# Five instead of four pairs of contraction tiles by seven products, in ten weight pairs of a two-layer trunk

## The chip, the cores and the metric

The kernel runs on one core of a Trainium2 chip. The metric is the device time of one execution in microseconds (us). The kernel before takes 1144.99 us, the median of three runs (1144.73 to 1146.62).

## The reference

The program computes two layers on x of 256 positions by 2048 columns, all in float32. Layer 1 normalizes x, projects it to three blocks of 4096 columns (u, v and a gate), mixes v over positions and projects back; layer 2 does the same with q, k, v and a gate (2048 columns each) and a causal attention.

```python
def gmlp_branch(xn, w_in, v_g, w_s, b_s, w_out):
    proj = xn @ w_in                                  # 2048 x 12288
    uv = jax.nn.gelu(proj[..., :2 * GMLP_WIDTH])
    zg = proj[..., 2 * GMLP_WIDTH:]
    u, v = jnp.split(uv, 2, axis=-1)
    v = rms_norm(v, v_g)
    ws = w_s * causal[None]
    mixed = einsum('gts,bnsgc->bntgc', ws, vc) + bias
    y = u * mixed * jax.nn.silu(zg)
    return y @ w_out                                  # 4096 x 2048

def stick_breaking_branch(xn, w_in, w_out):
    proj = xn @ w_in                                  # 2048 x 8192
    q, k, v, zg = jnp.split(proj, 4, axis=-1)
    o = stick_breaking_attention(q, k, v)
    return (o * jax.nn.silu(zg)) @ w_out              # 2048 x 2048

def reference(x, ...):
    h = x
    for i in range(2):
        h = h + branch_i(rms_norm(h, norm_g[i]), ...)
    return rms_norm(h, final_g)
```

## The kernel before, in words

**Tiles and cuts.** A product of activations with weights contracts over tiles of 128 rows of the weight matrix (16 of them where 2048 rows are contracted, 32 where 4096 are); its output is 128 positions by 512 columns, one PSUM bank, and the 256 positions are two halves (t = 0 and 1). Float32 operands go through TensorE as two float32r parts. `cut` (L108) makes them for up to two contraction tiles of 512 columns: ScalarE casts the raw tile to the high half `hi` (L114), VectorE subtracts this from the raw tile and writes the low half `lo` (L115). Two tiles are 128 x 1024 elements in one instruction, a single one 128 x 512. The halves lie in a pool of five buffers each. `terms` (L118) then issues three matmuls of 128 x 512: left high by hi (L119), left high by lo (L120), left low by hi (L121). A contraction tile for one half of the positions is thus three matmuls.

**Pairs.** The weights are worked on in pairs of column blocks of 512 (class `Pair`, L233): two v blocks, or the u and gate blocks that belong together, or q and k. Of the contraction tiles, `HALVES` puts some in a first half (0, 1, 2, 3, 8) and as many in a second (4, 5, 6, 7, 9). With positions, contraction halves and column blocks that gives a 2 x 2 by 2 x 2 block product, done by the seven products of a Strassen-Winograd scheme instead of eight. A pair's number `ks` (4 or 5) says how many tiles of each half take part: with 4 the groups are two of two tiles, with 5 there is a third group of one tile, the fifth tile. The seven products are called p1 to p7 and are worked off in the order p1, p5, p6, p2, p7, p3, p4. Each needs a cut per group and then 3 x `ks` matmuls. They go into banks called a, e, b, a, c, b and d, in that order.

In the code `b11` and `b12` are the first half's tiles of the first and second column block, `b21` and `b22` those of the second half. In the names of the instruction rows below, tiles are numbered from zero and groups last: `gu2_b00_1` is B11 of the third u/gate pair, group 1; `b01` is B12, `b10` B21, `b11` B22; group `_2` is the fifth tile. `gu2_p12_lo` is the low half of product p1, group 2.

Between the products the sums of weight tiles are made: two subtractions per group on VectorE (L286: B12 - B11 after p1, and B21 less the running sum after p6), one addition of B22 (L314, for groups 0 and 1), and additions of weight tiles from DRAM by accumulating DMAs from GpSimd's queue (`plus`, L294): B22 onto B12, and with a fifth tile also B22's fifth tile onto the running sum that p6 reads. `others` (L264) later loads the fifth tiles of B21 and B22 into the pool of plain raw tiles. VectorE also adds e into b and c (L334, L342).

The contraction tiles outside the halves (`rest`, 8 of 16 for four tiles, 6 for five) are done plainly, first for column block 0 (`column(0)`, within the pair), then for column block 1 (`column(1)`): per two tiles one load into a pool of three raw buffers (`wraw`), one cut, and 12 matmuls for both halves of the positions. The names are `gu2_010_raw` for column block 0, tiles 10 and 11, and `gu2_110_raw` for column block 1. `run` (L373) spreads the column 1 of a pair over the products p1, p5 and on of the next pair, so that the plain cuts of the one stand between the product cuts of the other. After a column's last matmul `evac` reads out its two banks.

**Left sides.** p5, p6, p7 and p3 take sums of the activations in place of a block. `Left.sums` (L134) makes them for four tiles per half, `Left.fifth` (L158) for the fifth: four VectorE additions of 128 x 128 per half and position (L165), four subtractions (L167 to L170), a cast, and one low half 128 x 512 (L172). Its intermediate sums are in two scratch buffers, `sg0` (`_full`) and `sg1` (`_sm`). For x they are called s0e and xs0e, and they are queued at the middle of the last v pair (L539); for the second layer's input xs1e, queued when the first column block of the o2 pair is done (L777).

**Order of the stages.** First a plain double block of v (pair 0), then v pairs 1 to 3 (named v2, v4, v6), eight u/gate pairs (gu0 to gu7) with the mixing of v between (`mixing`, L592: 6 matmuls more per pair, and VectorE's vl, L611, and wl, L605), the output projection (op0, o0, op1, o2), then q/k and v pairs of layer 2 (qk0 to qk3, bv0, bv2), two gate pairs and the last projection f. Of these, gu3, gu5 and the pairs from o2 on have five tiles, but for qk0, which has four; v1 to v3 and the other u/gate pairs have four.

**The order on each engine.** The program text gives the data flow; a list scheduler with a timeline model (`schedule_with_timeline_sim`) decides each engine's order at build time. Nearly all weight loads go through SyncE's queue (SP, L223), in the order in which they were scheduled, and each waits there until its target buffer is free, so that one late buffer holds up all loads behind it. Fifth tiles that `load` takes with `behind` follow the load before them. Two steps of the text concern the change further: for u/gate pairs `fifth_first=True` (L648, L244) puts the fifth group first in p1 and p5 and in the sums between (in all others it comes last), and qk0's head runs beside o2's column 1, seven steps of which go ahead (L815).

## Time and profile before

| what | value |
|---|---|
| median of three runs | 1144.99 us |
| profiled execution, span | 1142.0 us |
| TensorE matmul (PE) busy | 1132.3 us, 99% of the span, 5168 matmuls |
| TensorE weight load (PEld) busy | 937.6 us, 82% |
| VectorE (DVE) busy | 1010.9 us, 89%, 1111 instructions |
| ScalarE (ACT) busy | 828.5 us, 73%, 1102 instructions |
| GpSimd (POOL) busy | 99.8 us, 9% |
| DRAM read | 259.55 MB, with writes 231 GB/s over the span |

The span is the profiled execution's own time from its first to its last instruction; the median of the runs lies 3.0 us above it. The granted TensorE clock shows 1.00 in the windows that are quoted. In the windows that follow, a number stands for the busy time of an engine in that stretch, with the number of instructions behind the x. A row of the groups view gives an engine, an operation and its tiles, the count, the busy time with the mean of one in ns, and the idle time of the engine ahead of these instructions with what ended it. A row of the waits view is a waiting instruction, an arrow, what it waited for, and three numbers: the total wait in us, the number of waits, and the longest.

The eight u/gate pairs begin p7 (the first product into bank c) at 185.1, 227.2, 269.4, 313.8, 353.0, 397.5, 436.7 and 478.8 us, the three v pairs at 62.5, 103.5 and 144.3 us, and qk0 at 699.9 us.

### The profile page before, as it was taken

What the parts mean: (1) busy time and instruction counts of PE and PEld (TensorE: products, weight loads), DVE (VectorE), ACT (ScalarE), POOL (GpSimd) and SP (SyncE); (2) the same over time, 40 slices, a digit from 0 to 9 for tenths busy, and PEclk for the clock granted to TensorE, in tenths of its full rate; (3) what the DMA queues carried; (4) which work ended last, traced back from release to release, by engine and by line L of the source; (5) the groups of instructions that cost most, each with busy time, mean ns of one, the idle gap of its engine ahead of it and who ended that gap; (6) DMA issues with size and microseconds to landing.
All of it is one profiled execution on the core that took longest, in us unless ns stands there. A gap on an engine that the chain in (4) does not pass through costs nothing.

```text
span 1142.0 us, 14838 instructions
## 1 busy us (share of the span) xinstructions
PE 1132.3 (99%) x5168; PEld 937.6 (82%) x5168; DVE 1010.9 (89%) x1111; ACT 828.5 (73%) x1102; POOL 99.8 (9%) x106
## 2 busy tenths in 40 slices
...
GB/s 335 317 290 270 214 252 270 194 266 241 173 274 249 191 261 240 177 296 142 267 259 166 276 203 282 153 280 211 181 283 200 211 230 174 272 88 241 325 225 92
DMA packets 135659, 264.72 MB, mean 232 GB/s; under 512 B 8992, under 2 KB 9504, under 8 KB 135456
## 3 DMA queue, kind: packets, MB, share of 16 engines
...
q8 instruction: 40, 0.66, 0.2%
...
HBM read 259.55 MB, written 4.19 MB: 231 GB/s over the span
## 4 chain that ended last, share of the span: by engine, by line
PE 93%; DMA 2%; DVE 2%; issue 1%; ACT 1%; SPq 0%; POOLq 0%; POOL 0%; ACTq 0%; DVEq 0%
PE gu_a L119 3%; PE gu_b L119 3%; PE gu_b L121 3%; PE gu_a L121 3%; PE gu_a L120 3%; PE gu_b L120 3%; PE op_acc L119 2%; PE op_acc L120 2%; PE op_acc L121 2%; PE gu_d L119 2%; PE gu_d L121 2%; PE gu_c L121 2%; PE gu_d L120 2%; PE gu_c L119 2%; PE gu_c L120 2%; PE qk_a L121 1%
## 5 line engine op out<-in xcount | busy, mean ns | idle before, releaser
L114 ACT CAST gu_p_hi<-gu_b 128x1024 fp32r<-128x1024 f32 (+1 forms) x126 | 122.9, 1004 | 38.4 <-DVE gu_b L314 16.1
L115 DVE TENSOR_TENSOR gu_p_lo<-gu_b,gu_p_hi 128x1024 fp32r<-128x1024 f32 (+1 forms) x126 | 142.8, 1165 | 1.9 <-ACT gu_p_hi L114 1.2
L115 DVE TENSOR_TENSOR qk_p_lo<-qk_b,qk_p_hi 128x1024 fp32r<-128x1024 f32 (+1 forms) x77 | 80.8, 1073 | 8.9 <-ACT qk_p_hi L114 8.4
L114 ACT CAST qk_p_hi<-qk_b 128x1024 fp32r<-128x1024 f32 (+1 forms) x77 | 70.5, 934 | 19.0 <-DMA qk_b<-in_b_w_in 4.0
L115 DVE TENSOR_TENSOR gu_lo<-gu_raw,gu_hi 128x1024 fp32r<-128x1024 f32 x60 | 72.1, 1218 | 12.5 <-ACT gu_hi L114 12.2
L114 ACT CAST gu_hi<-gu_raw 128x1024 fp32r<-128x1024 f32 x60 | 62.0, 1052 | 21.0 <-DMA gu_raw<-in_a_w_in 11.5
L115 DVE TENSOR_TENSOR v_lo<-v_raw,v_hi 128x1024 fp32r<-128x1024 f32 (+1 forms) x41 | 48.9, 1193 | 15.2 <-ACT v_hi L114 15.2
L114 ACT CAST v_hi<-v_raw 128x1024 fp32r<-128x1024 f32 (+1 forms) x41 | 41.7, 1028 | 27.9 <-DMA v_raw<-in_a_w_in 26.4
L115 DVE TENSOR_TENSOR v_p_lo<-v_b,v_p_hi 128x1024 fp32r<-128x1024 f32 x42 | 50.3, 1220 | 3.3 <-ACT v_p_hi L114 3.1
L114 ACT CAST v_p_hi<-v_b 128x1024 fp32r<-128x1024 f32 x42 | 43.0, 1049 | 9.8 <-PE v_c L121 4.9
L115 DVE TENSOR_TENSOR bg_p_lo<-bg_b,bg_p_hi 128x1024 fp32r<-128x1024 f32 (+1 forms) x42 | 42.5, 1041 | 4.8 <-ACT bg_p_hi L114 4.7
L114 ACT CAST o_p_hi<-o_b 128x1024 fp32r<-128x1024 f32 (+1 forms) x35 | 33.4, 965 | 18.1 <-PE op_acc L121 13.0
L115 DVE TENSOR_TENSOR bv_p_lo<-bv_b,bv_p_hi 128x1024 fp32r<-128x1024 f32 (+1 forms) x42 | 42.5, 1040 | 3.8 <-ACT bv_p_hi L114 3.6
L114 ACT CAST bv_p_hi<-bv_b 128x1024 fp32r<-128x1024 f32 (+1 forms) x42 | 37.4, 908 | 10.0 <-DMA bv_b<-in_b_w_in 3.0
L294 POOL DMA_DIRECT2D gu_b<-in_a_w_in x20 | 23.0, 1155 | 240.2 <-DVE gu_b L286 134.3
L114 ACT CAST bg_p_hi<-bg_b 128x1024 fp32r<-128x1024 f32 (+1 forms) x42 | 37.3, 907 | 8.0 <-PE bg_a L121 2.5
L115 DVE TENSOR_TENSOR o_p_lo<-o_b,o_p_hi 128x1024 fp32r<-128x1024 f32 (+1 forms) x35 | 38.3, 1113 | 5.4 <-ACT o_p_hi L114 5.4
L286 DVE TENSOR_TENSOR gu_b<-gu_b,gu_b 128x1024 f32<-128x1024 f32 (+1 forms) x36 | 41.4, 1169 | 0.1
L114 ACT CAST o_hi<-o_raw 128x1024 fp32r<-128x1024 f32 x22 | 23.0, 1052 | 24.9 <-DMA o_raw<-in_a_w_out 24.8
L115 DVE TENSOR_TENSOR o_lo<-o_raw,o_hi 128x1024 fp32r<-128x1024 f32 x22 | 26.7, 1221 | 15.2 <-ACT o_hi L114 15.0
L114 ACT CAST op_hi<-op_raw 128x1024 fp32r<-128x1024 f32 x24 | 25.1, 1053 | 19.3 <-PE op_acc L121 8.8
L120 PE MATMUL op_acc<-op_lo,yc 128*128 128x512 f32 x96 | 37.8, 393 | 0.0
...
## 6 DMA issues: line engine op xcount, KB each, us to landing
...
```

What stands on the lines that cost most here:

```text
L114: nc.scalar.copy(hi[:, sl], raw[:, sl])
L115: low[0] = nc.vector.tensor_sub(lo[:, sl], raw[:, sl], f(hi[:, sl]))
L119: nc.tensor.matmul(acc, lh, hi, start=first, stop=False, skip_group_check=True)
L120: nc.tensor.matmul(acc, lh, lo, start=False, stop=False, skip_group_check=True)
L121: nc.tensor.matmul(acc, ll, hi, start=False, stop=last, skip_group_check=True)
L286: nc.vector.tensor_sub(into[g], b0[g], b1[g])
L294: adds.append(nc.gpsimd.dma_start(into[g], self.src(HALVES[i][k], n, j), accum_op=ALU.add))
```

## The change

Ten pairs go from four to five tiles per half: the v pairs 1 to 3 (`KS_A`), six of the eight u/gate pairs (`KS_GU`), and qk0. The left sums that go with four tiles stay as they are; the fifth sums of x, xs0e, are no longer queued in the last v pair but made right after the first four, ahead of v pair 1. The small pool `exg`, in which a pair's fifth tiles of B11 and B12 land, is opened ahead of the v pairs and closed behind the u/gate pairs. qk0 takes for its fifth tiles the scratch buffers `sg0` and `sg1`, as the o pairs do, and five instead of seven steps of o2's column 1 go ahead of its head.

```diff
@@ -17,8 +17,8 @@
 NEVER = -1e30
 CB = 512
 WARM = 9
-KS_A = 4
-KS_GU = (4, 4, 4, 5, 4, 5, 4, 4)
+KS_A = 5
+KS_GU = (5, 5, 5, 5, 5, 5, 5, 5)
 KS_B = 5
 KS_O = 5
 KS_F = 5
@@ -535,8 +535,6 @@
     def mid_v(b, pair):
         for i in (b - 2, b - 1):
             gain(i, pair)
-        if b == NV - 2:
-            queue.append((1, x_fifth))
 
     def x_fifth():
         with tc.issue_after(ins_of(low[0])):
@@ -557,7 +555,10 @@
         if i < 3:
             square(2 + 2 * i)
             square(3 + 2 * i)
-    left.sums(KS_A, home("xs", [P, 2, 4, KS_A, P], F32R, "xs0"), "s0")
+    left.sums(4, home("xs", [P, 2, 4, 4, P], F32R, "xs0"), "s0")
+    x_fifth()
+    lx = ctx.enter_context(ExitStack())
+    ex = lx.enter_context(tc.tile_pool(name="exg", bufs=1))
     pending.append(p0.column(1))
     prior.append(KD // 4)
     for b in range(2, NV, 2):
@@ -585,7 +586,6 @@
         return py.tile([P, 2, 2, S], F32R, tag="yc3", bufs=2, name=f"yc3_{k2}")
 
     with ExitStack() as lg:
-        ex = lg.enter_context(tc.tile_pool(name="exg", bufs=1))
         pb = lg.enter_context(tc.tile_pool(name="pb", bufs=2))
         rv = None
 
@@ -649,6 +649,7 @@
         flush()
         drain()
         prior.clear()
+    lx.close()
     pv.close()
 
     hs = ctx.enter_context(tc.tile_pool(name="hs", bufs=1, space=bass.MemoryType.DRAM)).tile([P, NT, D], F32, name="hs")
@@ -810,9 +811,10 @@
     tail = p.column(1)
     while len(queue) > TPB // 2:
         queue.pop(0)[1]()
-    p = Pair(columns(b_w_in, 0, D), left1, KD, "qk0", 4, lambda j, t, bank: evac_qk(0, j, t, bank),
-             mid=lambda pair: drain())
-    for _ in range(7):
+    p = Pair(columns(b_w_in, 0, D), left1, KD, "qk0", KS_B, lambda j, t, bank: evac_qk(0, j, t, bank),
+             mid=lambda pair: drain(),
+             fifth=lambda j, name: jk.tile([P, 1, CB], F32, tag=f"sg{j}", bufs=1, name=name))
+    for _ in range(5):
         next(tail)
     drain()
     for _ in p.head():
```

Per converted pair, the seven products grow from 84 to 105 matmuls and from 14 cuts to 21 (14 of two tiles, 7 of one); the rest shrinks from 8 tiles to 6, 96 matmuls to 72 and 8 cuts to 6. Two subtractions of 128 x 512 come on VectorE (L286), two accumulating DMAs of 256 KB on GpSimd's queue (L294), and four loads of one tile (256 KB) in place of two loads of two (512 KB).

Three places show how the order moves. **The first** is SyncE's queue between two u/gate pairs. Before, between gu1 and gu2, both of four tiles:

```order
L223 DMA gu1_08_raw_2127<-in_a_w_in 128x2x512
L223 DMA gu1_010_raw_2145<-in_a_w_in 128x2x512
L223 DMA gu1_012_raw_2163<-in_a_w_in 128x2x512
L223 DMA gu2_b10_0_2340<-in_a_w_in 128x2x512
L223 DMA gu2_b10_1_2342<-in_a_w_in 128x2x512
L223 DMA gu2_b01_0_2209<-in_a_w_in 128x2x512
L223 DMA gu2_b01_1_2211<-in_a_w_in 128x2x512
L223 DMA gu2_b11_0_2270<-in_a_w_in 128x2x512
L223 DMA gu2_b11_1_2272<-in_a_w_in 128x2x512
L223 DMA gu2_b00_0_2205<-in_a_w_in 128x2x512
L223 DMA gu2_b00_1_2207<-in_a_w_in 128x2x512
L223 DMA gu1_014_raw_2181<-in_a_w_in 128x2x512
```

With the change, at the turn from gu2 to gu3, both of five tiles:

```order
L223 DMA gu3_b10_0_2842<-in_a_w_in 128x2x512
L223 DMA gu3_b10_1_2844<-in_a_w_in 128x2x512
L223 DMA gu2_012_raw_2686<-in_a_w_in 128x2x512
L223 DMA gu3_b01_0_2736<-in_a_w_in 128x2x512
L223 DMA gu3_b01_1_2738<-in_a_w_in 128x2x512
L223 DMA gu3_b11_0_2786<-in_a_w_in 128x2x512
L223 DMA gu3_b11_1_2788<-in_a_w_in 128x2x512
L223 DMA gu2_014_raw_2704<-in_a_w_in 128x2x512
L223 DMA gu3_b00_0_2730<-in_a_w_in 128x2x512
L223 DMA gu3_b00_1_2732<-in_a_w_in 128x2x512
L223 DMA gu3_b01_2_2734<-in_a_w_in 128x512
L223 DMA gu3_b00_2_2728<-in_a_w_in 128x512
```

The third plain load of column 0 (before `gu1_012_raw`, now `gu2_014_raw`) moved from ahead of the next pair's loads to behind its second tile of B22 (`gu3_b11_1`); the next pair's two fifth tiles stand at the end of its head's loads.

On VectorE at the same turn, before (gu1 to gu2):

```order
L605 TENSOR_TENSOR wl1_2107<-ws1_2104,wh1_2106 128x256
L115 TENSOR_TENSOR gu1_08_lo_2130<-gu1_08_raw_2127,gu1_08_hi_2129 128x1024
L115 TENSOR_TENSOR gu1_010_lo_2148<-gu1_010_raw_2145,gu1_010_hi_2147 128x1024
L115 TENSOR_TENSOR gu1_012_lo_2166<-gu1_012_raw_2163,gu1_012_hi_2165 128x1024
L611 SCALAR_TENSOR_TENSOR vl2_2467<-v0_113,nv_r_1739,vh2_2466 128x512 x2
L115 TENSOR_TENSOR gu1_014_lo_2184<-gu1_014_raw_2181,gu1_014_hi_2183 128x1024
L115 TENSOR_TENSOR gu2_p10_lo_2215<-gu2_b00_0_2205,gu2_p10_hi_2214 128x1024
L115 TENSOR_TENSOR gu1_18_lo_2227<-gu1_18_raw_2224,gu1_18_hi_2226 128x1024
L286 TENSOR_TENSOR gu2_b00_0_2205<-gu2_b01_0_2209,gu2_b00_0_2205 128x1024
```

and now (gu2 to gu3):

```order
L605 TENSOR_TENSOR wl2_2648<-ws2_2645,wh2_2647 128x256
L115 TENSOR_TENSOR gu2_p42_lo_2638<-gu2_b00_2_2348,gu2_p42_hi_2637 128x512
L115 TENSOR_TENSOR gu2_010_lo_2671<-gu2_010_raw_2668,gu2_010_hi_2670 128x1024
L115 TENSOR_TENSOR gu2_012_lo_2689<-gu2_012_raw_2686,gu2_012_hi_2688 128x1024
L115 TENSOR_TENSOR gu2_014_lo_2707<-gu2_014_raw_2704,gu2_014_hi_2706 128x1024
L611 SCALAR_TENSOR_TENSOR vl3_3033<-v0_113,nv_r_1875,vh3_3032 128x512 x2
L115 TENSOR_TENSOR gu3_p12_lo_2742<-gu3_b00_2_2728,gu3_p12_hi_2741 128x512
L286 TENSOR_TENSOR gu3_b00_2_2728<-gu3_b01_2_2734,gu3_b00_2_2728 128x512
L115 TENSOR_TENSOR gu3_p10_lo_2749<-gu3_b00_0_2730,gu3_p10_hi_2748 128x1024
L115 TENSOR_TENSOR gu3_p11_lo_2759<-gu3_b00_1_2732,gu3_p11_hi_2758 128x1024
L286 TENSOR_TENSOR gu3_b00_0_2730<-gu3_b01_0_2736,gu3_b00_0_2730 128x1024
```

There are three plain cuts of column 0 instead of four, and behind the factors vl3 the next pair now starts with its fifth tile's cut and subtraction (`gu3_p12_lo`, `gu3_b00_2`) ahead of its first two-tile cut (`gu3_p10_lo`).

**The second** is VectorE at the start of v pair 1, beside column 1 of pair 0. Before:

```order
L115 TENSOR_TENSOR v0_014_lo_402<-v0_014_raw_399,v0_014_hi_401 128x1024
L115 TENSOR_TENSOR v2_p10_lo_448<-v2_b00_0_442,v2_p10_hi_447 128x1024
L115 TENSOR_TENSOR v0_18_lo_460<-v0_18_raw_457,v0_18_hi_459 128x1024
L286 TENSOR_TENSOR v2_b00_0_442<-v2_b01_0_475,v2_b00_0_442 128x1024
L115 TENSOR_TENSOR v2_p11_lo_480<-v2_b00_1_444,v2_p11_hi_479 128x1024
L286 TENSOR_TENSOR v2_b00_1_444<-v2_b01_1_477,v2_b00_1_444 128x1024
L115 TENSOR_TENSOR v0_110_lo_492<-v0_110_raw_489,v0_110_hi_491 128x1024
L115 TENSOR_TENSOR v2_p50_lo_517<-v2_b00_0_442,v2_p50_hi_516 128x1024
L314 TENSOR_TENSOR v2_b00_0_442<-v2_b11_0_507,v2_b00_0_442 128x1024
```

Now:

```order
L115 TENSOR_TENSOR v0_014_lo_402<-v0_014_raw_399,v0_014_hi_401 128x1024
L165 TENSOR_TENSOR s0e_full_443<-x0_hi_111,x0_lo_112 128x128 x4
L115 TENSOR_TENSOR v2_p10_lo_466<-v2_b00_0_458,v2_p10_hi_465 128x1024
L115 TENSOR_TENSOR v2_p11_lo_482<-v2_b00_1_460,v2_p11_hi_481 128x1024
L169 TENSOR_TENSOR s0e_sm_444<-s0e_full_443 128x128
L115 TENSOR_TENSOR v2_p12_lo_492<-v2_b00_2_462,v2_p12_hi_491 128x512
L167 TENSOR_TENSOR s0e_sm_444<-s0e_full_443 128x128
L286 TENSOR_TENSOR v2_b00_0_458<-v2_b01_0_475,v2_b00_0_458 128x1024
L286 TENSOR_TENSOR v2_b00_1_460<-v2_b01_1_477,v2_b00_1_460 128x1024
L286 TENSOR_TENSOR v2_b00_2_462<-v2_b01_2_479,v2_b00_2_462 128x512
L168 TENSOR_TENSOR s0e_sm_444<-s0e_full_443,s0e_sm_444 128x128
L115 TENSOR_TENSOR v0_18_lo_501<-v0_18_raw_498,v0_18_hi_500 128x1024
```

The sums of the fifth tiles of x (`s0e_full`, `s0e_sm`) stand among the cuts of p1, and column 1's first plain cut, `v0_18_lo`, moved behind all of p1's cuts and the three subtractions.

**The third** is qk0 beside column 1 of o2. SyncE's queue before:

```order
L223 DMA o2_124_raw_5938<-in_a_w_out 128x2x512
L223 DMA o2_126_raw_5966<-in_a_w_out 128x2x512
L223 DMA o2_128_raw_6003<-in_a_w_out 128x2x512
L223 DMA o2_130_raw_6031<-in_a_w_out 128x2x512
L223 DMA qk0_08_raw_6224<-in_b_w_in 128x2x512
L223 DMA qk0_010_raw_6242<-in_b_w_in 128x2x512
```

and now:

```order
L223 DMA o2_126_raw_6223<-in_a_w_out 128x2x512
L223 DMA o2_128_raw_6251<-in_a_w_out 128x2x512
L223 DMA qk0_b00_2_6112<-in_b_w_in 128x512
L223 DMA qk0_b01_2_6118<-in_b_w_in 128x512
L223 DMA o2_130_raw_6276<-in_a_w_out 128x2x512
L223 DMA qk0_b10_2_6391<-in_b_w_in 128x512
```

Two loads of fifth tiles, `qk0_b00_2` and `qk0_b01_2`, stand ahead of o2's last plain load. On VectorE now:

```order
L115 TENSOR_TENSOR o2_122_lo_6162<-o2_122_raw_6159,o2_122_hi_6161 128x1024
L170 TENSOR_TENSOR xs1e_sm_6043<-xs1e_full_6042,xs1e_sm_6043 128x128
L172 TENSOR_TENSOR xs1e_6041<-xs1e_sm_6043,xs1e_6041 128x512
L115 TENSOR_TENSOR qk0_p12_lo_6178<-qk0_b00_2_6112,qk0_p12_hi_6177 128x512
L286 TENSOR_TENSOR qk0_b00_2_6112<-qk0_b01_2_6118,qk0_b00_2_6112 128x512
L115 TENSOR_TENSOR o2_124_lo_6187<-o2_124_raw_6184,o2_124_hi_6186 128x1024
L115 TENSOR_TENSOR qk0_p50_lo_6214<-qk0_b00_0_6108,qk0_p50_hi_6213 128x1024
```

The fifth tile's cut and subtraction follow directly behind the last of the fifth sums `xs1e`, and the next plain cut of o2 stands behind them.

## The prediction

> **What bounds the kernel now.** I read the page first, then who waited for whom, with TensorE alone, then windows of about one pair each (from the first product into bank c of one pair to that of the next), then timelines.
>
> ```profile
> PE wps L79 <- DVE warm L76: 1.3, 1, 1.3
> PE v_acc L120 <- DVE v_lo L115: 0.6, 1, 0.6
> PE gT L434 <- ACT bsg L1011: 0.2, 1, 0.2
> PE v_acc L119 <- ACT v_hi L114: 0.2, 1, 0.2
> core 0: us, PE busy (x) PEld busy (x) DVE busy (x) ACT busy (x) POOL busy (x), PEclk, DMA share, GB/s
> 185.10:227.20 42.10, 42.10 (x187) 34.88 (x186) 41.55 (x45) 33.82 (x41) 6.02 (x5) 1.00 0.79 232
> 313.80:353.00 39.20, 39.20 (x174) 32.47 (x173) 37.01 (x38) 32.00 (x41) 5.66 (x4) 1.00 0.79 238
> 353.00:397.50 44.50, 44.50 (x198) 36.83 (x197) 41.22 (x44) 32.73 (x41) 5.83 (x6) 1.00 0.81 233
> 436.70:478.80 42.10, 42.10 (x187) 34.81 (x186) 39.03 (x39) 32.12 (x38) 4.31 (x4) 1.00 0.71 215
> ```
>
> Three TensorE rows of the timeline, with two dense rows of VectorE (the second number is how long, x4 four instructions end to end):
>
> ```profile
> 433.95 0.39 PE L119 MATMUL gu_a<-gu_p_hi,x_hi 128*128 128x512 f32 x1
> 439.39 0.39 PE L119 MATMUL gu_b<-gu_p_hi,xs 128*128 128x512 f32 x1
> 439.62 0.40 PE L120 MATMUL gu_b<-gu_p_lo,xs 128*128 128x512 f32 x1
> 438.24 4.61 DVE L115 TENSOR_TENSOR gu_p_lo<-gu_b,gu_p_hi 128x1024 fp32r<-128x1024 f32 x4
> 227.22 4.62 DVE L115 TENSOR_TENSOR gu_p_lo<-gu_b,gu_p_hi 128x1024 fp32r<-128x1024 f32 x4
> 230.17 0.39 PE L120 MATMUL gu_b<-gu_p_lo,xs 128*128 128x512 f32 x1
> ```
>
> TensorE waits for others 2.3 us in the whole run, so it bounds the kernel: from 433.95 to 439.39 lie 24 matmuls, 0.2267 us each. But VectorE is close behind, busy 39 of 42 us. How close is its **lead**: when the low half of a cut is ready before TensorE first reads it. In the same product of a pair, the first low half of the dense VectorE row ends at 227.22 + 1.22 = 228.44 and is read at 230.17 in the second u/gate pair (1.7 us ahead), and ends at 439.46 and is read at 439.62 in the seventh, which follows a five-tile pair (0.2 us ahead). One five-tile pair between four-tile ones has used up nearly all slack. That is the place to work out.
>
> **The change, part by part.** Removed on TensorE: 3 matmuls in each of ten pairs (12 x 5 tiles less 105, against 12 x 4 less 84), 30 x 0.2267 = 6.8 us. A v pair goes from 180 x 0.2267 = 40.8 to 40.1, a u/gate pair (6 mixing matmuls with it) from 42.2 to 41.5.
>
> Added on VectorE, per pair: seven cuts and two subtractions 512 wide, for two cuts 1024 wide less.
>
> ```profile
> L115 DVE TENSOR_TENSOR gu_p_lo<-gu_b,gu_p_hi 128x1024 fp32r<-128x1024 f32 x28 | 33.6, 1220 | 0.4 <-ACT gu_p_hi L114 0.2
> L115 DVE TENSOR_TENSOR gu_lo<-gu_raw,gu_hi 128x1024 fp32r<-128x1024 f32 x14 | 16.8, 1217 | 3.4 <-ACT gu_hi L114 3.3
> L115 DVE TENSOR_TENSOR gu_p_lo<-gu_b,gu_p_hi 128x512 fp32r<-128x512 f32 x7 | 5.0, 715 | 0.0
> L611 DVE SCALAR_TENSOR_TENSOR vl<-v,nv_r,vh 128x512 fp32r<-128x512 f32 x4 | 2.8, 746 | 1.7 <-ACT vh L610 1.7
> L605 DVE TENSOR_TENSOR wl<-ws,wh 128x256 fp32r<-128x256 f32 x2 | 0.8, 413 | 0.0
> ```
>
> ```profile
> 684.80 1.22 DVE L115 TENSOR_TENSOR qk_p_lo<-qk_b,qk_p_hi 128x1024 fp32r<-128x1024 f32 x1
> 685.93 1.22 DVE L115 TENSOR_TENSOR o_lo<-o_raw,o_hi 128x1024 fp32r<-128x1024 f32 x1
> 695.17 0.68 DVE L695 TENSOR_TENSOR h<-o_b,h 128x512 f32<-128x512 f32 x1
> 695.77 0.68 DVE L695 TENSOR_TENSOR h<-o_c,h 128x512 f32<-128x512 f32 x1
> ```
>
> The first five rows are VectorE's groups from 313.8 to 397.5, one five-tile and one four-tile pair. Packed, an instruction starts 685.93 - 684.80 = 1.13 us (1.135 over longer rows) after a 1024-wide one and 0.60 after a 512-wide one: 0.08 less than each lasts. I cost by starts. A four-tile u/gate pair has 28 wide ones (14 cuts of products, 8 plain cuts, 6 sums of weight tiles), six 512-wide (two adds of e, four factors), two of vl (0.746 - 0.08 = 0.66) and one of wl (0.33): 37.0 us. A five-tile pair has 26 wide and 9 + 6 narrow: 40.1 us. Together 77.1; the two windows say 37.01 + 41.22 = 78.2. So each conversion adds 3.1 us to VectorE while TensorE gives up 0.7, and a five-tile pair leaves VectorE 41.5 - 40.1 = 1.4 us for waits.
>
> **Waits it cannot shed.**
>
> ```profile
> 313.94 5.83 DVE L115 TENSOR_TENSOR gu_p_lo<-gu_b,gu_p_hi 128x1024 fp32r<-128x1024 f32 x6 [0.22 <-ACT gu_p_hi L114]
> 326.58 1.23 DVE L115 TENSOR_TENSOR gu_lo<-gu_raw,gu_hi 128x1024 fp32r<-128x1024 f32 x1 [1.86 <-ACT gu_hi L114]
> 410.63 1.23 DVE L115 TENSOR_TENSOR gu_lo<-gu_raw,gu_hi 128x1024 fp32r<-128x1024 f32 x1 [2.28 <-ACT gu_hi L114]
> 325.50 1.05 ACT L114 CAST gu_hi<-gu_raw 128x1024 fp32r<-128x1024 f32 x1 [2.83 <-DMA gu_raw<-in_a_w_in]
> 318.66 0.37 SPq L223 DMA_DIRECT2D gu_raw<-in_a_w_in  x1
> gu_b<-in_a_w_in SPq DMA_DIRECT2D x8, 256.0 KB, 6.0
> gu_b<-in_a_w_in POOLq DMA_DIRECT2D x4, 256.0 KB, 6.5
> L294 POOL DMA_DIRECT2D gu_b<-in_a_w_in x20 | 23.0, 1155 | 240.2 <-DVE gu_b L286 134.3 <-DMA gu_raw<-in_a_w_in 54.2 <-ACT v L481 34.7
> ```
>
> In both five-tile pairs VectorE stands 1.9 and 2.3 us at the third plain cut of column 0. Its load stands in SP's queue behind the next pair's second tile of B22, whose buffer VectorE itself frees with the second cut of p3 (the fourth of six in the row at 313.94, so it ends near 318.0). Issued at 318.66, the load lands at 325.50, and VectorE starts on it at 326.58, 8.6 us after that cut, with 6.7 us of work between (cuts of p3 and p4, two wide and two narrow; the add to c; wl; two plain cuts). The loop starts and ends on VectorE, so being late does not shorten it: 2.1 us per pair. In the change the next pair has a fifth tile too, and uses it first. Its load stands behind that third raw tile and two loads of B11, the last of which waits for the cuts of p4: issued some 5.0 us after the same cut of p3, landed 6.0 later, cast in 0.6, it is there at 11.6 to 11.8. VectorE wants it behind the third plain cut and vl, at 8.6 + 1.13 + 1.33 = 11.1: 0.6 more. So 40.1 + 2.1 + 0.6 = 42.8 us for a five-tile pair after another, where TensorE needs 41.5. Bounds: 41.5, if another order swallows the waits, to 44.4, if the wait for the accumulated fifth tile before p6 (6.5 us landing) and a third raw of 2.3 come whole. I take 42.8, since two pairs of this trace show its larger part. Ahead of it stand the lead of 1.7 - 0.2 = 1.5 us, spent once.
>
> u/gate: six pairs go from 42.2 to 42.8 (+3.6), the two that were at five from 41.5 to 42.8 (+2.6), and the first carries four gains more (4 x 0.60), of which some 1.5 us fit into its wait (+0.9). **+7.1.** v pairs 2 and 3: 26 wide, 9 + 6 narrow, 38.5 us; the gains stand between the raw cuts and fill all but 1.0 of that wait, but here the fifth group comes last in p5, and its accumulation (1.2 to issue, 6.5 to land, 0.6 to cast) meets only 5 wide instructions, 1.6 us short; 41.1 against 40.8, **+0.6** for both.
>
> v pair 1 also takes the fifth sums.
>
> ```profile
> 40.35 1.22 DVE L115 TENSOR_TENSOR v_lo<-v_raw,v_hi 128x1024 fp32r<-128x1024 f32 x1 [1.81 <-ACT v_hi L114]
> 671.78 0.28 DVE L165 TENSOR_TENSOR xs1e_full<-x 128x128 f32<-128x128 f32 x1
> 671.98 0.48 DVE L719 SCALAR_TENSOR_TENSOR x<-hT,cols,x 128x256 fp32r<-128x256 f32 x1
> 48.00:54.00 6.00, 6.00 (x28) 4.99 (x27) 6.00 (x6) 4.45 (x6) 0.04 (x1) 1.00 1.10 265
> ```
>
> They are eight instructions 128 wide at 0.2 us and one at 0.6: 2.2 us, moved out of the stage at 150 to 185 into one where VectorE and the DMA engines are full (6.00 of 6.00, share over 1). Up to the end of p7 VectorE gets 2.2 + 7 x 0.6 = 6.4 us more, TensorE 15 x 0.2267 = 3.4; the one gap, 1.81, hides that much, so TensorE stands 1.2. The loads that stand before column 1's first plain cut grow by 0.5 MB, up to 1.9 us at 265 GB/s; I take a stall of 1.6; with 0.7 saved, **+0.9** (bounds -0.7 to +2.4).
>
> First q/k pair: its fifth tile now lands in the scratch buffer of the fifth sums.
>
> ```profile
> 677.18 0.28 DVE L170 TENSOR_TENSOR xs1e_sm<-xs1e_full,xs1e_sm 128x128 f32<-128x128 f32 x1
> 678.52 0.68 DVE L172 TENSOR_TENSOR xs1e<-xs1e_sm,xs1e 128x512 fp32r<-128x512 f32 x1
> qk_b<-in_b_w_in SPq DMA_DIRECT2D x12, 256.0 KB, 5.1
> ```
>
> The load can start only when the row at L170 has read that buffer, takes 5.1 us and a cast, and its low half stands two instructions behind L170 on VectorE, with the plain cuts of the o pair's column behind it. From L170 it is some 0.5 to issue, 5.1, 0.6 and 0.6 to the low half, 6.8 us, of which TensorE has 2.7 in the twelve matmuls of the plain cut before, and its lead: a stall of 4.1 without lead, of none with 4 us of it. I take the middle, 2.0, less 0.7 saved: **+1.3** (bounds -0.7 to +3.4).
>
> The 5 MB of extra loads (0.5 per pair) I cost at nothing where the share is 0.8, outside these loops. ScalarE gains some 2 us a pair and is busy 32 of 42. Sum: 7.1 + 0.6 + 0.9 + 1.3 - 1.5 = **+8.4 us**; span 1142.0 to 1150.4. The median 1144.99 is 3.0 above that span, so **1153.4 us**.
>
> **Rivals.** (1) TensorE stays the bound: another order hides the loops, and the 6.8 us come off, less some 1 to 2 for the first v and the q/k pair: 1140. For it: the trace has no stalled pair yet, and later stages with five tiles in a row run without TensorE waiting. Against it: there a pair has more matmuls beside it. It wins if VectorE's waits per pair stay under 1.4 us. (2) Both about cancel, waits of some 2 us a pair: 1145. (3) Everything that VectorE gets is on the path: 10 x 3.1 = 31 us, 1176. Against it: TensorE has no waits now, so 1.5 us of lead and the difference of 42.2 to 37.0 must be used up first.
>
> The Trainium skill (Perfetto Trace Analysis, Identifying the Most-Contended Engine) judges TensorE by its weight loads' busy share and the others by occupancy. By that rule VectorE, 39.03 of 42.10, already leads TensorE, 34.81, which speaks for (3); the wait rows disagree for the kernel before, and I follow them.
>
> **How the numbers follow.** Forecast (VectorE's loop sets the u/gate pairs) 0.70, its own range 1147 to 1164; rival 1 0.15; rival 2 0.11; rival 3 0.04. 0.2% is 2.3 us, about what this measurement can tell from no change. Faster 0.17 (rival 1 and a part of 2), same 0.11, slower 0.72. The range goes from rival 1's upper edge, 1141, to 1163, where 44 us per pair would bring it.
>
> **What would show it.** TensorE waits on VectorE's low halves, 1 to 2 us in each u/gate pair, where there were none; VectorE over 95% busy from 185 to 480 with a wait of about 2 us at each third plain cut; pairs of 42.5 to 43.5 us; a wait of some us at the first q/k pair's third cut. If pairs come out at 41.5 us with VectorE waiting for TensorE, the forecast is wrong, and the loops are not what I take them for.

## The result, and the profile after

The change made the kernel **slower**: 1181.46 us (median of four runs, 1177.09 to 1185.78) against 1145.76, a ratio of 1.031 with a 95% interval of 1.0281 to 1.0338. That is 36 us, where the prediction had 8.4 us and a range up to 1163. The profiled execution took 1181.14 us, with a span of 1179.4 against 1142.0.

TensorE waited 2.3 us in the kernel before. The waits view of the changed kernel for TensorE (total, count, longest, in us) now has these five rows on top:

```profile
PE v_acc L119 <- ACT v_hi L114: 4.7, 3, 3.7
PE v_b L119 <- ACT v_hi L114: 4.1, 3, 3.1
PE qk_a L119 <- ACT qk_p_hi L114: 3.5, 1, 3.5
PE gu_b L120 <- DVE gu_p_lo L115: 2.6, 10, 0.4
PE gu_c L120 <- DVE gu_p_lo L115: 2.5, 6, 0.5
```

There are two kinds. The first three rows are single waits of 3 to 4 us for a cast of ScalarE; the last two are many short ones for VectorE's low halves. Windows show where they lie: v pair 1, which has no pair ahead of it, from 46 us on, and then, each from the first product into bank c of one pair to that of the next, v pair 3, two u/gate pairs and the first q/k pair, which follows o2:

```profile
core 0: us, PE busy (x) PEld busy (x) DVE busy (x) ACT busy (x) POOL busy (x), PEclk, DMA share, GB/s
46.00:71.20 25.20, 20.89 (x80) 16.41 (x79) 19.10 (x20) 14.11 (x19) 2.05 (x4) 0.86 0.84 229
112.30:158.40 46.10, 42.39 (x179) 34.20 (x178) 40.10 (x43) 30.92 (x44) 5.36 (x6) 0.96 0.79 236
374.80:418.80 44.00, 42.98 (x184) 33.95 (x183) 40.97 (x45) 33.08 (x43) 5.89 (x6) 1.00 0.79 231
418.80:462.70 43.90, 43.00 (x185) 33.98 (x184) 40.98 (x45) 33.20 (x43) 5.69 (x6) 1.00 0.78 231
647.50:738.90 91.40, 87.67 (x387) 71.84 (x386) 71.18 (x87) 50.64 (x69) 4.14 (x4) 0.98 0.70 210
```

The u/gate pairs take 43.9 us on average, v pair 3 takes 46.1, and in three stages the granted clock is under 1.00, which no part of the prediction had. I worked out the loss from the distances between the starts of matmuls: what exceeds 0.2267 us, for distances over 0.25. By stage (us from the span's start) this is 6.3 (30 to 95), 4.5 (138 to 175), 2.8 (175 to 205, the entry to the u/gate pairs), 16.8 (205 to 520) and 6.1 (680 to 760). Beside these stand 25 matmuls at 0.427 us in three of the stages, 5.0 us. With some 7 us spread over the rest of the run it is 48.4 from 30 us on, against 6.4 before; less 6.8 us of matmuls taken off, that makes 35.2 of the 37.4 us by which the span grew. Most of the rest are distances under 0.25.

**The clock.** Windows around the first long wait, and TensorE's rows in it and behind it (start, duration):

```profile
56.00:58.00 2.00, 0.00 (x0) 0.00 (x0) 0.00 (x0) 1.05 (x2) 0.00 (x0) 0.57 1.11 261
58.00:60.00 2.00, 1.96 (x5) 1.57 (x6) 1.98 (x2) 0.94 (x1) 0.00 (x0) 0.50 1.06 315
60.00:62.00 2.00, 2.00 (x6) 1.57 (x5) 2.00 (x3) 1.84 (x3) 0.00 (x0) 0.50 0.73 252
60.77 0.63 PE L119 MATMUL v_b<-v_p_hi,xs 128*128 128x512 f32 x1
61.20 0.63 PE L120 MATMUL v_b<-v_p_lo,xs 128*128 128x512 f32 x1
64.41 0.40 PE L119 MATMUL v_acc<-v_hi,x_hi 128*128 128x512 f32 x1
64.64 0.39 PE L120 MATMUL v_acc<-v_lo,x_hi 128*128 128x512 f32 x1
```

TensorE stood idle for 3.7 us up to 58.05; in that time the clock fell to 0.50 and stayed there to 63.1. Matmuls start 0.427 us apart (60.77 to 61.20), and 0.23 when it is back. The same follows the idle stretches of 3.1 us (up to 150.42) and 3.5 us (up to 714.03). A busy share of 1.00 in such a window tells nothing: at half clock TensorE is as "busy" with half the work. The Trainium skill (TensorE: Matmul & The Clock Gate, Part 1: The HAM clock gate) says that the clock is halved after an idle window of about 3.4 us and comes back after a busy one, with windows that run freely. The traces agree with the windows: in those of both kernels and of all fifteen runs every stretch of one clock lasts a whole multiple of 3.413 us, here 6.83 behind this wait and 3.41 behind the next. They do not agree that a whole window must be idle. I cut the stretches at full clock into windows of that length and added up TensorE's idle time in each (the ends of matmuls are modelled, so 0.1 us either way). The clock fell behind every window with 1.9 us of idle time or more, six within the runs and the rest at their ends, and behind no window with 1.69 or less. The three waits here left 2.60, 1.96 and 1.98 us in one window. So it also matters how a wait falls on the windows.

**The third plain cut of a u/gate pair**, VectorE's timeline in a settled pair:

```profile
387.95 2.35 DVE L115 TENSOR_TENSOR gu_lo<-gu_raw,gu_hi 128x1024 fp32r<-128x1024 f32 x2
392.18 1.23 DVE L115 TENSOR_TENSOR gu_lo<-gu_raw,gu_hi 128x1024 fp32r<-128x1024 f32 x1 [1.88 <-ACT gu_hi L114]
393.95 1.42 DVE L611 SCALAR_TENSOR_TENSOR vl<-v,nv_r,vh 128x512 fp32r<-128x512 f32 x2 [0.55 <-ACT vh L610]
395.86 0.69 DVE L115 TENSOR_TENSOR gu_p_lo<-gu_b,gu_p_hi 128x512 fp32r<-128x512 f32 x1 [0.49 <-ACT gu_p_hi L114]
```

VectorE waits 2.92 us in a pair (for the third raw tile, for the factors' cast, for the next pair's fifth tile) and works 40.97; together that is the pair's 43.9.

**The three long waits.** v pair 1, in the rows of SyncE's queue, GpSimd and ScalarE:

```profile
40.82 4.75 SPq L223 DMA_DIRECT2D v_raw<-in_a_w_in  x2
42.53 3.54 POOL L294 DMA_DIRECT2D v_b<-in_a_w_in  x3 [3.36 <-ACT v L481]
56.95 1.04 ACT L114 CAST v_hi<-v_raw 128x1024 fp32r<-128x1024 f32 x1 [6.97 <-DMA v_raw<-in_a_w_in]
```

A plain raw tile of pair 0's column 1 is asked for at 40.82 and is there only 16 us later; three accumulating transfers start behind it and run beside it (share 1.1). In the kernel before, the same tile stood ahead of the two loads of B21; there it was asked for at 37.19 and took 10 us:

```profile
37.19 4.78 SPq L223 DMA_DIRECT2D v_raw<-in_a_w_in  x2
```

That the order decides shows in `e9_v_both` below; that the accumulating transfers are what slows the tile is likely, but no run tells them apart from the other loads. v pair 3:

```profile
141.40 0.85 POOL L294 DMA_DIRECT2D v_b<-in_a_w_in  x1 [2.20 <-DVE v_p_lo L115]
148.80 0.62 ACT L114 CAST v_p_hi<-v_b 128x512 fp32r<-128x512 f32 x1 [4.92 <-DMA v_b<-in_a_w_in]
149.32 1.04 ACT L114 CAST v_hi<-v_raw 128x1024 fp32r<-128x1024 f32 x1
150.42 0.50 PE L119 MATMUL v_b<-v_hi,x_hi 128*128 128x512 f32 x1 [3.06 <-ACT v_hi L114]
```

The accumulated fifth tile that p6 reads is asked for at 141.40 and cast at 148.80. The next plain tile had landed at 133.9, but its cast stands behind the late one in ScalarE's order (149.32 behind 148.80), and TensorE, which had that tile's matmuls in hand to bridge the wait, stops with it. The first q/k pair:

```profile
705.30 0.28 DVE L170 TENSOR_TENSOR xs1e_sm<-xs1e_full,xs1e_sm 128x128 f32<-128x128 f32 x1
705.82 1.50 SPq L223 DMA_DIRECT2D qk_b<-in_b_w_in  x2
713.36 0.62 ACT L114 CAST qk_p_hi<-qk_b 128x512 fp32r<-128x512 f32 x1 [7.12 <-DMA qk_b<-in_b_w_in]
714.01 0.69 DVE L115 TENSOR_TENSOR qk_p_lo<-qk_b,qk_p_hi 128x512 fp32r<-128x512 f32 x1 [7.05 <-ACT qk_p_hi L114]
```

From the sum that frees the scratch buffer to the low half it is 8.7 us, and VectorE stands for 7.05 of them.

### The profile page after: what moved, and what is told of

It is laid out like the page before. It is cut to its first block, busy times and chain, and to the rows that moved or that the text cites. A ratio compares the mean times of both kernels' runs of the same rounds, so it can differ in the third digit from the quotient of the medians.

```text
span 1179.4 us, 15050 instructions
## 1 busy us (share of the span) xinstructions
PE 1144.7 (97%) x5138; PEld 931.6 (79%) x5138; DVE 1042.4 (88%) x1181; ACT 845.0 (72%) x1152; POOL 120.4 (10%) x126
## 4 chain that ended last, share of the span: by engine, by line
PE 53%; DVE 17%; DMA 15%; issue 7%; ACT 7%; SPq 1%; POOL 0%; ACTq 0%; POOLq 0%; DVEq 0%
DVE gu_p_lo L115 6%; DMA gu_b<-in_a_w_in 5%; DMA v_raw<-in_a_w_in 3%; ACT gu_p_hi L114 2%; DVE gu_b L286 2%; DMA o_raw<-in_a_w_out 2%; DMA v_b<-in_a_w_in 2%; PE op_acc L121 2%; PE op_acc L120 2%; PE op_acc L119 2%; DVE v_p_lo L115 1%; DVE gu_lo L115 1%; DMA gu_raw<-in_a_w_in 1%; PE f_acc L121 1%; PE f_acc L119 1%
## 5 line engine op out<-in xcount | busy, mean ns | idle before, releaser
L114 ACT CAST gu_p_hi<-gu_b 128x1024 fp32r<-128x1024 f32 (+1 forms) x168 | 145.5, 906 | 53.1 <-DVE gu_b L314 21.5
L115 DVE TENSOR_TENSOR gu_p_lo<-gu_b,gu_p_hi 128x1024 fp32r<-128x1024 f32 (+1 forms) x168 | 169.3, 1044 | 7.1 <-ACT gu_p_hi L114 6.8
L114 ACT CAST gu_hi<-gu_raw 128x1024 fp32r<-128x1024 f32 x48 | 49.5, 1048 | 31.1 <-DMA gu_raw<-in_a_w_in 20.7
L115 DVE TENSOR_TENSOR gu_lo<-gu_raw,gu_hi 128x1024 fp32r<-128x1024 f32 x48 | 57.9, 1217 | 15.7 <-ACT gu_hi L114 15.6
L115 DVE TENSOR_TENSOR v_p_lo<-v_b,v_p_hi 128x1024 fp32r<-128x1024 f32 (+1 forms) x63 | 63.2, 1040 | 7.7 <-ACT v_p_hi L114 7.7
L114 ACT CAST v_p_hi<-v_b 128x1024 fp32r<-128x1024 f32 (+1 forms) x63 | 55.5, 904 | 16.4 <-DMA v_b<-in_a_w_in 9.7
L294 POOL DMA_DIRECT2D gu_b<-in_a_w_in x32 | 33.4, 1066 | 251.5 <-ACT gu_p_hi L114 170.8
L115 DVE TENSOR_TENSOR v_lo<-v_raw,v_hi 128x1024 fp32r<-128x1024 f32 (+1 forms) x35 | 41.8, 1196 | 12.9 <-ACT v_hi L114 12.7
L286 DVE TENSOR_TENSOR gu_b<-gu_b,gu_b 128x1024 f32<-128x1024 f32 (+1 forms) x48 | 50.0, 1044 | 0.4
L115 DVE TENSOR_TENSOR bg_p_lo<-bg_b,bg_p_hi 128x1024 fp32r<-128x1024 f32 (+1 forms) x42 | 42.5, 1042 | 4.8 <-ACT bg_p_hi L114 4.7
L114 ACT CAST bv_p_hi<-bv_b 128x1024 fp32r<-128x1024 f32 (+1 forms) x42 | 37.4, 907 | 10.5 <-PE bv_a L121 2.3
L294 POOL DMA_DIRECT2D qk_b<-in_b_w_in x16 | 16.7, 1078 | 215.7 <-DVE qk_b L286 106.3
L121 PE MATMUL op_acc<-op_hi,yc 128*128 128x512 f32 x96 | 37.5, 393 | 0.0
```

What stands on the lines that cost most here:

```text
L114: nc.scalar.copy(hi[:, sl], raw[:, sl])
L115: low[0] = nc.vector.tensor_sub(lo[:, sl], raw[:, sl], f(hi[:, sl]))
L121: nc.tensor.matmul(acc, ll, hi, start=False, stop=last, skip_group_check=True)
L286: nc.vector.tensor_sub(into[g], b0[g], b1[g])
L294: adds.append(nc.gpsimd.dma_start(into[g], self.src(HALVES[i][k], n, j), accum_op=ALU.add))
```

## The experiments

In the diffs `...` stands for text that is left out. The times are medians beside a kernel before of 1144.9 to 1145.6 us on the same chip; each ratio is to it, with its 95% interval.

### One part of the change at a time

`e1_gu_only` is the kernel before with `KS_GU` at five throughout:

```diff
-KS_GU = (4, 4, 4, 5, 4, 5, 4, 4)
+KS_GU = (5, 5, 5, 5, 5, 5, 5, 5)
```

> Only the eight u/gate pairs at five tiles; v pairs, x's fifth sums and the first q/k pair as before. Theory (VectorE's loop through the third plain load sets every five-tile pair): pairs of 43.5 to 44 us from the second on, TensorE's waits some 2.3 us in each, none long enough for the clock to drop; 13 to 15 us over the kernel before. Rival (the u/gate pairs were only late because the v pairs handed them over without lead, and would recover): pairs of 41.5 to 42.5 us, 0 to 4 us over the kernel before.

Measured: 1164.04 us, ratio 1.0158 (1.0142 to 1.0173), so +18.8. Pairs of 43.7 to 46.1 us from the second on, with the granted clock at 1.00. The theory's mechanism holds, its sum was 4 us short: the pairs are longer than in the whole change, since VectorE waits more for the third raw tile:

```profile
336.96 1.23 DVE L115 TENSOR_TENSOR gu_lo<-gu_raw,gu_hi 128x1024 fp32r<-128x1024 f32 x1 [2.55 <-ACT gu_hi L114]
318.90:363.50 44.60, 43.30 (x184) 33.84 (x183) 40.97 (x45) 33.12 (x43) 5.89 (x6) 1.00 0.78 226
```

`e2_v_only` is the changed kernel with `KS_GU` and the q/k pair as before:

```diff
-KS_GU = (5, 5, 5, 5, 5, 5, 5, 5)
+KS_GU = (4, 4, 4, 5, 4, 5, 4, 4)
-    p = Pair(..., "qk0", KS_B, ..., fifth=lambda j, name: jk.tile(..., tag=f"sg{j}", ...))
-    for _ in range(5):
+    p = Pair(..., "qk0", 4, ...)
+    for _ in range(7):
```

> Only the three v pairs at five tiles with x's fifth sums made early; u/gate counts (4,4,4,5,4,5,4,4) and the first q/k pair as before. Theory (two single late transfers, a plain raw tile in v pair 1 and the accumulated fifth tile in v pair 3, each with a stretch at half clock behind it): 10 to 14 us over the kernel before, TensorE idle 3 to 4 us near 55 and near 148 us, granted clock 0.5 behind each. Rival (VectorE as a whole is too full in v pairs): many small waits, all three pairs longer by 3 to 4 us, no clock drop.

Measured: 1155.50 us, ratio 1.0085 (1.0066 to 1.0105), +10.3. The theory holds for v pair 1 (TensorE idle for 3.5 us near 55 us, 13 matmuls at half clock behind it). In v pair 3 TensorE stood idle for 2.3 us, and there the clock did not fall (the idle time fell on two windows, 1.21 and 1.09 us):

```profile
58.00:60.00 2.00, 1.74 (x4) 1.45 (x5) 1.76 (x2) 1.16 (x2) 0.00 (x0) 0.50 1.09 298
146.00:152.00 6.00, 3.70 (x17) 2.75 (x16) 3.85 (x4) 2.73 (x4) 0.00 (x0) 1.00 0.60 161
152.00:156.00 4.00, 4.00 (x19) 3.31 (x18) 4.00 (x5) 3.60 (x6) 0.00 (x0) 1.00 0.60 156
```

`e3_qk_only` is the kernel before with the change's edit of the first q/k pair:

```diff
-    p = Pair(..., "qk0", 4, ...)
-    for _ in range(7):
+    p = Pair(..., "qk0", KS_B, ..., fifth=lambda j, name: jk.tile(..., tag=f"sg{j}", ...))
+    for _ in range(5):
```

> Only the first q/k pair at five tiles, its fifth tiles in the scratch buffers of the fifth sums. Theory (the load can't start until the sums have read that buffer): TensorE idle 3 to 4 us at the pair's start, half clock for some 3.4 us behind it, 6 to 7.5 us over the kernel before. Rival (the stall was a consequence of the u/gate stage's delay): 0 to 2 us over.

Measured: 1152.38 us, ratio 1.0064 (1.0043 to 1.0086), +7.2; one wait, with 3.6 us between two starts, and matmuls at 0.427 us behind it. As the theory has it. The three parts make 18.8 + 10.3 + 7.2 = 36.3 us; the change alone, 36. **They add up**, so each can be looked at by itself.

`e4_early_sums` makes x's fifth sums early, with all counts as before:

```diff
     left.sums(4, home("xs", [P, 2, 4, 4, P], F32R, "xs0"), "s0")
+    x_fifth()
+    lx = ctx.enter_context(ExitStack())
+    ex = lx.enter_context(tc.tile_pool(name="exg", bufs=1))
```

> All pairs with their old number of tiles; only x's fifth sums are made ahead of v pair 1 and the small pool is opened earlier. Theory (the late raw tile in v pair 1 comes from the order and number of the loads of a five-tile pair): within 1.5 us of the kernel before. Rival (the fifth sums' 2.2 us on VectorE cause v pair 1's stall): 4 to 8 us over, TensorE idle 2 us or more between 50 and 60 us.

Measured: 1144.71 us, ratio 0.9993 (0.9984 to 1.0003). The early sums cost nothing; v pair 1 was late for its loads.

### The u/gate loop, one wait at a time

All of these have only the u/gate pairs at five tiles. `e5_third_early` gives the third plain raw tile of column 0 two idle buffers of a later stage (`yc3`), so that its load need not wait for p3's cuts:

```diff
-                raw = wraw.tile([P, 2, CB], F32, tag="raw", ...)
+                pool, tag = (py, "yc3") if self.third and j == 0 and i == 4 else (wraw, "raw")
+                raw = pool.tile([P, 2, CB], F32, tag=tag, bufs=2 if pool is py else None, ...)
```

> Only the u/gate pairs at five tiles, and the third plain raw tile of column 0 has two buffers of its own (idle ones of a later stage), so that its load is issued a pair earlier. Theory (two waits in series on one loop: behind the third raw tile stands the next pair's fifth tile, whose load can be issued only after p4's last cut): VectorE's wait at the third plain cut goes from 2.6 us to 0, the wait at the fifth tile's cut grows from 0.5 to some 3 us, pairs stay at 43.5 to 44.5 us, within 4 us of the same kernel without the early load (1164.0). Rival (the third raw tile alone is the bound): pairs of 41.5 to 42 us, 1146 to 1150.

`e6_fifth_twice` gives the fifth tiles of B11 and B12 two buffers each:

```diff
-        ex = lg.enter_context(tc.tile_pool(name="exg", bufs=1))
-        pb = lg.enter_context(tc.tile_pool(name="pb", bufs=2))
+        ex = lg.enter_context(tc.tile_pool(name="exg", bufs=2))
+        pb = lg.enter_context(tc.tile_pool(name="pb", bufs=1))
```

> Only the u/gate pairs at five tiles, and the fifth tiles of B11 and B12 have two buffers each (those of the mixing one instead of two), so that their loads no longer wait for p4's cut. Theory (two waits in series): the wait at the fifth tile's cut goes, the one at the third plain cut stays at 2 to 2.6 us, pairs of 43 to 44 us, 1158 to 1163. Rival (the fifth tile is the bound): pairs of 41.5 to 42 us, 1146 to 1150.

`e7_both` has both edits.

> Only the u/gate pairs at five tiles, with both: the third plain raw tile loaded a pair earlier, and two buffers for each fifth tile. Theory (the loop consists of these two waits, and VectorE's own work of 40.5 to 41 us a pair is less than TensorE's 41.5): VectorE without waits over 0.5 us at either place, pairs of 41.5 to 42.2 us, 1143 to 1150. Rival (VectorE's amount of work is the bound, the waits are only where its slack shows): TensorE goes on waiting 2 us a pair for low halves, 1158 to 1164.

Measured: `e5` 1165.05 us, ratio 1.0177 (1.0162 to 1.0193); `e6` 1159.22, 1.0119 (1.0104 to 1.0135); `e7` 1155.45, 1.0092 (1.0077 to 1.0107). VectorE's rows at the place of the waits, first of `e5`, then of `e6`, then of `e7`:

```profile
334.83 3.49 DVE L115 TENSOR_TENSOR gu_lo<-gu_raw,gu_hi 128x1024 fp32r<-128x1024 f32 x3
339.28 1.41 DVE L613 SCALAR_TENSOR_TENSOR vl<-v,nv_r,vh 128x512 fp32r<-128x512 f32 x2 [0.96 <-ACT vh L612]
342.41 0.69 DVE L115 TENSOR_TENSOR gu_p_lo<-gu_b,gu_p_hi 128x512 fp32r<-128x512 f32 x1 [1.72 <-ACT gu_p_hi L114]
```

```profile
333.75 1.22 DVE L115 TENSOR_TENSOR gu_lo<-gu_raw,gu_hi 128x1024 fp32r<-128x1024 f32 x1 [1.93 <-ACT gu_hi L114]
```

```profile
336.74 0.69 DVE L287 TENSOR_TENSOR gu_b<-gu_b,gu_b 128x512 f32<-128x512 f32 x1 [1.36 <-DMA gu_b<-in_a_w_in]
```

In `e5` the three plain cuts run through without a wait, and VectorE waits for the fifth tile and the factors instead (1.72 and 0.96): pairs of 43.7 and 44.4 us, nothing gained. In `e6` the wait for the third raw tile stays, pairs of 43.2. Both are as the theory of two waits in series says. `e7` lies between the theory and its rival: with both gone, VectorE waits at the subtraction for the fifth tile of B12 (L286 of the kernel before), 1.1 to 2.1 us in a pair, and pairs take 42.3 to 43.3 us. **A third wait stood behind the two.** That load, though its buffer was free, was kept behind the load before it by `load`'s `behind`. `e11_all_three` lets it go ahead:

```diff
-                load(raw, self.src(HALVES[i][k], n, j), behind=g >= 2)
+                load(raw, self.src(HALVES[i][k], n, j), behind=g >= 2 and not self.third)
```

> Only the u/gate pairs at five tiles; the third raw tile early, two buffers for each fifth tile, and the fifth tile of B12 no longer kept behind the load before it, so that it too is loaded a pair earlier. Theory (in the kernel without this last part, at 1155.4, VectorE still waited 1.1 to 2.1 us a pair for that tile): this wait goes, pairs of 41.5 to 42.2 us against 42.8, 1148 to 1152 (the entry from the v pairs, some 3 us late, stays). Rival (VectorE's amount of work is now the bound): pairs stay at 42.6 to 43 us, 1154 to 1157.

Measured: 1151.36 us, ratio 1.0056 (1.0042 to 1.0071). Two pairs in the windows of this kernel:

```profile
323.30:364.80 41.50, 41.50 (x185) 34.31 (x184) 40.58 (x45) 33.54 (x43) 6.23 (x6) 1.00 0.82 244
364.80:406.30 41.50, 41.50 (x185) 34.34 (x184) 40.61 (x45) 33.39 (x43) 6.15 (x6) 1.00 0.82 244
```

From the fourth pair on each takes **41.5 us** (the first three 41.8 to 43.2) and in these windows TensorE waits for nothing. VectorE does the same work (40.6 of 41.5 us) as when the pair took 44. So VectorE's amount of work was never the bound here; its waits on a loop through the loads were. The Trainium skill (Perfetto Trace Analysis, Optimization Strategy) says that the same gap, repeating on an engine that should be full, can mean too few buffers for the next tile; here VectorE's gap at the third plain cut, some 2 us in every pair, was that, and so was the one at the fifth tile behind it; the third was not, for there the buffer was free and the order of loads held the tile up. The 6 us that remain came from elsewhere: the tiles with free buffers had been loaded among the program's first loads, and TensorE lost 14.0 us in the first 75 us, against 4.9 before. One of the waits there, of 2.0 us (67.80 to 70.20), fell into one window of the clock and halved it from 70.6 to 74.0:

```profile
PE v_c L119 <- ACT v_c L332: 2.0, 1, 2.0
60.00:90.00 30.00, 27.98 (x115) 22.36 (x114) 24.56 (x25) 19.11 (x25) 0.00 (x0) 0.94 0.83 278
```

The profiled execution was the slowest of the four (1154.98 us), so not all of this need be in the median. `e13_gu_start` keeps the first two pairs' extra tiles behind the load before them:

```diff
+                load(..., behind=pool is py and not self.free)
-                load(..., behind=g >= 2 and not self.third)
+                load(..., behind=g >= 2 and not self.free)
+            p.third, p.free = b < NV - 1, b > 1
```

> As the run with pairs of 41.5 us (u/gate pairs alone at five tiles, third raw tile early, two buffers per fifth tile), but the first two pairs' extra tiles are kept behind the load before them, so that they are not loaded at the start of the program. Theory (what was left, 6 us, came from these loads among the first ones): TensorE's waits before 75 us are back to some 4 us, pairs stay at 41.5 us, 1141 to 1145. Rival (the u/gate stage itself costs it): 1149 or more.

Measured: 1146.53 us, ratio 1.0013 (1.0003 to 1.0023): above the theory's range by 1.5 us, far below the rival's. The waits ahead of 75 us are gone and the pairs stay at 41.5, but some 4 us of waits lie at the entry to the stage and in its first pairs, partly for x's fifth sums (0.9 us in one row), and they eat the 4.1 us of matmuls saved.

### The three long waits

`e9_v_both` is `e2_v_only` with two edits:

```diff
-        steps = (3 if len(pair.groups) > 2 else 2) * len(pair.groups)
+        steps = (3 if len(pair.groups) > 2 and pair.name != "v2" else 2) * len(pair.groups)
-                 ..., mid=lambda pair: mid_v(b, pair))
+                 ..., mid=lambda pair: mid_v(b, pair), fifth_first=b > 2)
```

> Only the three v pairs at five tiles with early fifth sums, and two changes: column 1 of pair 0 is spread over six steps of v pair 1's head instead of nine, so that its raw tiles stand ahead of the loads of B21; v pairs 2 and 3 take their fifth group first in p1 and p5, so that the accumulated fifth tile is asked for earlier. Theory (two late transfers, each with half clock behind it): both stalls gone, no stretch at half clock, 1144 to 1149. Rival (DMA engines too full in this stage whatever the order): TensorE still idle 2 to 4 us between 50 and 60 us, 1150 or more.

Measured: 1149.61 us, ratio 1.0043 (1.0026 to 1.0060), 0.6 us over the theory's range: both long waits and the half clock are gone (5.9 us below `e2_v_only`), but short waits of 7.4 us in all stay between 30 and 155 us, against 1.25 before. The longest rows of TensorE there:

```profile
PE v_acc L120 <- DVE v_lo L115: 0.8, 2, 0.5
PE v_acc L119 <- ACT v_hi L114: 0.6, 1, 0.6
```

`e10_qk_own` is `e3_qk_only` with a buffer of its own for the first of the two fifth tiles, and the subtraction that needs the other one moved behind p5's second cut:

```diff
-             fifth=lambda j, name: jk.tile([P, 1, CB], F32, tag=f"sg{j}", ...))
+             fifth=lambda j, name: (po, jk)[j].tile([P, 1, CB], F32, tag=("f5", "sg0")[j], ...))
-            self.minus(self.b11, self.b12, self.b11, self.early)
+            self.minus(self.b11, self.b12, self.b11, (0, 1) if split else self.early)
...
+                if split and g == 1:
+                    with tc.issue_after(ins_of(low[0])):
+                        self.minus(self.b11, self.b12, self.b11, (2,))
+                    self.plus(self.b12, 1, 1, 2)
```

> Only the first q/k pair at five tiles; its fifth tile of B11 has a buffer of its own, so that its load is issued long before the pair, and its fifth tile of B12 (still in the scratch buffer) is subtracted after p5's second cut instead of before p5. Theory (the scratch buffer alone makes the stall): TensorE's wait at p1's third cut goes from 3.5 us to under 0.5, no half clock, 1143.5 to 1147. Rival (the wait moves to the subtraction of the other fifth tile, which holds up VectorE behind it): TensorE idle 1 to 3 us some 8 us later, 1147 to 1150.

Measured: 1146.08 us, ratio 1.0008 (0.9999 to 1.0017). VectorE cuts the fifth tile right behind the sum that held it up before, and no long wait and no half clock is left in this stage:

```profile
677.47 0.28 DVE L170 TENSOR_TENSOR xs1e_sm<-xs1e_full,xs1e_sm 128x128 f32<-128x128 f32 x1
677.67 0.68 DVE L115 TENSOR_TENSOR qk_p_lo<-qk_b,qk_p_hi 128x512 fp32r<-128x512 f32 x1
```

The buffer made the stall. The 0.7 us of matmuls saved don't show: the interval holds no change.

`e12_filled` is `e3_qk_only` with 16 matmuls into a spare bank in the stall:

```diff
+                if self.name == "qk0" and nm == "p1" and g == 2:
+                    spare = ps_ms.tile([P, CB], F32, tag="ms", name="spare")
+                    lh, ll = part(0)
+                    for _ in range(16):
+                        with tc.issue_after(ins_of(tail_mm[0])):
+                            tail_mm[0] = nc.tensor.matmul(spare, lh, old, start=True, stop=True, ...)
```

> Only the first q/k pair at five tiles with its fifth tiles in the scratch buffers, as in the run of 1152.4, and 16 extra matmuls into a spare bank (their result is not used) that stand directly ahead of the matmuls which wait: TensorE works 3.6 us through the stall. Theory (the idle time is what halves the clock): no matmul at 0.427 us behind the stall, granted clock 1.00 throughout, 0.5 to 2 us below that run. Rival (the clock drops for another reason at this place): matmuls at 0.427 us stay, time not below 1152.

Measured: 1151.54 us, ratio 1.0060 (1.0045 to 1.0074). On TensorE and in a window behind the stall (added lines shift the line numbers):

```profile
680.77 3.79 PE L284 MATMUL spare<-qk_p_hi,x 128*128 128x512 f32 x16
685.26 0.50 PE L122 MATMUL qk_a<-qk_p_hi,x 128*128 128x512 f32 x1 [0.71 <-ACT qk_p_hi L115]
688.00:690.00 2.00, 2.00 (x9) 1.65 (x10) 2.00 (x3) 2.00 (x4) 0.11 (x1) 1.00 0.45 71
```

The wait ends at the same point of the work, but in the profiled execution the clock stays at 1.00 and no matmul takes 0.427 us: the idle time is what halves the clock. (Two of the six executions have a mean clock of 0.996 instead of 0.999, so a fall in those is not excluded.) The time came out 0.8 us below `e3_qk_only`, and the two intervals overlap, so the gain itself is not shown.

### The whole change with all of it mended, and a search for a faster version

`e14_all_mended` is the changed kernel with the edits of `e9`, `e10` and `e11` together, the third raw tile and the fifth tiles of v pairs 2 and 3 in buffers of their own too.

> The whole change, all ten pairs at five tiles, with every late transfer mended: third raw tiles and fifth tiles of the v pairs 2 and 3 and of the u/gate pairs in buffers of their own, the raw tiles of v pair 1 ahead of B21, the fifth group first in v pairs 2 and 3, the q/k pair's first fifth tile in its own buffer. Theory (the four transfers, and the half clock behind three of them, are the whole cause): 6.8 us of matmuls come off and 1 to 4 us of waits stay, 1139 to 1143, faster than the kernel before. Rival (VectorE's 31 us more or the 5 MB more cost something whatever the order): 1146 or more.

Measured: 1148.84 us, ratio 1.0028 (1.0018 to 1.0038). The mended transfers take away 32 of the change's 36 us (0.0310 - 0.0028 of the time before). But it is 6 us over the theory's range and still slower than before: by its number the rival has it, which leaves its cause open. Its remaining waits for TensorE lie in the v stage:

```profile
PE v_acc L119 <- ACT v_hi L114: 1.9, 3, 0.8
PE v_b L119 <- ACT v_hi L114: 1.8, 2, 1.1
PE v_acc L120 <- DVE v_lo L115: 0.9, 2, 0.6
PE v_a L119 <- ACT v_p_hi L114: 0.9, 2, 0.4
```

By the distances of the matmuls it is 7.8 us from 30 to 155 us (1.25 before), more than all ten conversions save (6.8). Three of the longer waits (at 63.8, 103.3 and 144.8 us; 0.6, 0.9 and 1.2 us) again stand behind the cast of the accumulated fifth tile, for which ScalarE waited 3.4, 1.2 and 1.6 us. So part of the remainder is still a late transfer.

`e15_gu_from_1` and `e16_gu_early` try to keep the gain of the mended u/gate stage, one with the first pair at four tiles, one with the early fifth sums:

```diff
-KS_GU = (5, 5, 5, 5, 5, 5, 5, 5)
+KS_GU = (4, 5, 5, 5, 5, 5, 5, 5)
```

> v pairs and the first q/k pair as before; u/gate pairs at (4, 5, 5, 5, 5, 5, 5, 5) tiles with the third raw tile early and two buffers per fifth tile. Theory (entry waits for the fifth sums were what ate the gain): no wait at the entry, pairs of 41.5 us from the second on, 3.4 us of matmuls less, 1141 to 1144. Rival (the extra bytes and VectorE work push the waits elsewhere): within 1 us of the kernel before.

> v pairs and the first q/k pair as before in their number of tiles; all eight u/gate pairs at five tiles with the third raw tile early and two buffers per fifth tile, and x's fifth sums made ahead of v pair 1. Theory: the waits for the fifth sums (1.9 us in the run at 1146.5) go, 1142 to 1145. Rival (they go to v pair 1 or to the plain cuts at the entry): within 1 us of that run, 1145.5 to 1147.5.

Measured: 1144.80 us, ratio 0.9992 (0.9980 to 1.0004), and 1146.38, ratio 1.0004 (0.9992 to 1.0016). The rivals hold: the waits moved to the first pairs (5.3 us from 190 to 520 us in the one, 3.6 in the other, against 0.5 before). No version here is faster than the kernel before by more than the measurement can tell.

## Why the prediction was wrong

The direction was right; the size was a quarter of the measured one, and the range ended 18 us too low. Of the signs that it named, three came: 2 us at the third plain cut, short waits for low halves of some 2.3 us a pair, and a wait at the q/k pair's third cut. Two did not: VectorE was busy 93 to 94% from 185 to 480 us, not over 95%, and pairs took 43.9 us, not 42.5 to 43.5. The steps that failed are the size of the u/gate loop, the loads of the v pairs, the landing time in the q/k pair, and the clock, which was not in the sum at all. By the terms:

- **u/gate, +7.1 and -1.5 of lead: measured +18.8 alone.** The step named the right loop: `e5`, `e6`, `e7` and `e11` take its waits away one after the other, and the pair goes from 44.6 to 41.5 us only when the last is gone. Mis-sized were two things. VectorE's work is 40.97 us a pair, not 40.1; the check in the prediction itself (78.2 in the windows against 77.1 counted) showed 0.55 of this per pair, and I passed over it. And the waits are 2.9 us in the changed kernel and 3.5 in `e1`, not 2.7: the wait for the factors' cast (0.55 and 0.42) was not in the sum, and the third raw tile is 2.55 us late in `e1` instead of 2.1, while the two forecast waits came out a bit smaller in the changed kernel (1.88 + 0.49). That makes 43.9 to 44.6 us, near the upper bound that I had set (44.4), eight times over. That bound alone would have brought the time to 1166; the range ended at 1163, for 44 us a pair, and the upper bounds of the other terms were not added to it.
- **v pairs, +0.6 and +0.9: measured +10.3.** For v pair 1 the step named the wrong cause: the fifth sums are free (`e4`). What it missed is the order of loads. Column 1 of pair 0 is spread over nine steps instead of four, which puts its last raw tiles behind B21's loads, and so among the accumulating transfers; the extra bytes at 265 GB/s were priced, the one tile that takes 16 us was not. For v pair 3 the step had the right wait, the accumulated fifth tile 1.6 us late, but priced it as VectorE's time in the pair (38.5 + 1.0 + 1.6 = 41.1 against 40.8), where the pair's slack took up nearly all of it. VectorE stood 2.7 us for it, and TensorE 3.1 at that place, as the plain matmuls that could have bridged it stand behind the late cast on ScalarE; slack elsewhere in the pair does not help there. In v pair 2, with the same order, TensorE lost 0.9 us.
- **First q/k pair, +1.3: measured +7.2.** Mechanism right, shown by `e10`. The term that was too small is the load, 7.4 us to land instead of 5.1. The lead was about what I took: TensorE worked on for 5.2 us behind the sum at 705.30, which is the 2.7 us of the plain cut and a lead of 2.5. The wait of 3.5 us and 1.6 us of half clock behind it make 5.1 of the 7.2; the rest are short waits behind them.
- **The clock was missing altogether.** It stood at nothing, without a reason. Behind each of the three long waits 7 to 10 matmuls ran at 0.427 us, 1.4 to 2.0 us on top (13 and 2.6 us in `e2`). The kernel before had no such wait past its start, so nothing in its profile priced it.
- **The rivals.** Rival 1 (1140) is what the u/gate stage does once mended, 41.5 us a pair, though even then the gain is lost around it. Rival 3 (1176, everything VectorE gets is on the path) came nearest in time, and for a reason that the runs deny: in `e11` VectorE does the same extra work at no cost. The same run goes against the rule of the Trainium skill (Perfetto Trace Analysis, Identifying the Most-Contended Engine), by which the engine with the highest occupancy is the most contended, with TensorE judged by its weight loads: in `e11` VectorE is busy 40.6 of 41.5 us, above TensorE's 34.3 by weight loads, and TensorE has no waits.

Settled is that the three parts add up, which transfer is late in each, and that mending them takes away 32 of 36 us. Not settled is the remainder in the v stage: part of it is still the accumulated fifth tile, and whether the rest is VectorE's extra work or the extra loads there, no run tells apart.
